# Hybrid attention layer: compressed values' product in fp32r, y made where z is made, the prelude's transposes in another order

## The chip, the core and the metric

The kernel runs on one core of one Trainium2 chip. The metric is the time of one execution on the device in microseconds, lower being better. The core has TensorE (PE, whose weight loads are shown as PEld), VectorE (DVE), ScalarE (ACT), GpSimd (POOL) and SyncE (SP), which issues the transfers (DMA). PSUM holds what PE writes, SBUF holds everything else on the chip.

## What is computed

One decoder layer on a sequence of 512 tokens of width 1024 in float32: a normalisation modulated by a condition c, one wide projection, two groups of attention heads (A: sliding window with sinks; B: three branches over compressed, selected and windowed keys), a gate by SiLU of z, and an output projection added to x.

```python
# D_MODEL 1024, SEQ 512, BATCH 1, HEAD_DIM 64; 8 heads in each group, 2 K/V heads (g) with 4 query heads (r) each
mod = jax.nn.silu(c) @ w_ada + b_ada
shift, scale, gate = jnp.split(mod, 3, axis=-1)
h = rms_norm(x, norm_gain) * (1 + scale[:, None, :]) + shift[:, None, :]
proj = h @ w_in
(q_a, k_a, v_a, z_a, q_b, kc, vc, ks, vs, kw, vw, z_b, g_b) = jnp.split(proj, _split_points(), axis=-1)
...
o_a = banded_gqa(qa, ka, heads(v_a, A_KV), SWA_WINDOW, rel_bias[:, :A_HEADS], sinks)
...
k_cmp = qk_norm(compress_blocks(heads(kc, B_KV), cmp_pos_k, w_cmp_k1, w_cmp_k2), k_gain_cmp)
v_cmp = compress_blocks(heads(vc, B_KV), cmp_pos_v, w_cmp_v1, w_cmp_v2)
...
o_cmp, o_sel = nsa_cmp_sel(qb, k_cmp, v_cmp, k_sel, heads(vs, B_KV), bias_b)
o_win = banded_gqa(qb, k_win, heads(vw, B_KV), NSA_WINDOW, bias_b, None)
gb = jax.nn.sigmoid((g_b + b_nsa_gate).astype(jnp.float32)).reshape(Bn, S, B_HEADS, N_NSA_BRANCHES, 1)
o_b = gb[..., 0, :] * o_cmp + gb[..., 1, :] * o_sel + gb[..., 2, :] * o_win

y = jnp.concatenate([o_a.reshape(Bn, S, D_A) * jax.nn.silu(z_a.astype(jnp.float32)),
                     o_b.reshape(Bn, S, D_B) * jax.nn.silu(z_b.astype(jnp.float32))], axis=-1)
out = y.astype(x.dtype) @ w_out
return x + gate[:, None, :] * out
```

Group B's compressed branch takes 31 overlapping blocks of 32 tokens, runs each through a small MLP to one key and one value of 64 elements per K/V head g, and attends to these. With 512 tokens there are 8 blocks to select from and 16 may be selected, so the selected branch attends to all earlier tokens.

## The kernel before

**Stages.** A prelude up to about 49 us loads x, turns it (x has 4 blocks of 128 tokens; each is transposed on PE in two halves of four 128x128 pieces), computes the modulation, and runs the first projection (q, k and v of group A) over eight blocks k of the model width. From there to about 268 us two streams are interleaved: slots of attention, one for each head row, branch and query block, and the remaining projections, done in pieces in between (L490, L500). Last comes the output projection, eight column blocks n of 24 matmuls with 512 columns (L500; the last n in two halves), each followed by one DVE operation for gate and residual (L1048) and a store.

**Precision.** The large products run in fp32r. Where that is not enough, an operand is split in two fp32r parts, a high part that is its rounded copy and a low part that is what rounding left out, and two or three products are added in PSUM. So weights are split by ACT (wh, L175) and DVE (wl, L176), h into hh and hl, y into yh and yl. Products in plain fp32 are shown in the trace as two records each.

**The compressed branch.** `cmp_mlp` ends in the second layer: keys in one product, values by L648 (four fp32 matmuls, two K/V heads by two halves of the hidden width), where the 32 value rows stand four times below each other in a tile `vc[g]` of 128 rows. `cmp_attn` makes the probabilities and transposes them (L714) into two tables `PTc[g]` (L716), in which rows 32r to 32r+32 belong to head row r. `slot_pv` collects a head row's output `o` in one PSUM bank: the probabilities times values of its slots (L969) and, for group B after the last slot of a head row, the compressed values' product: for each g one fp32 matmul (L975) with 32 rows and 64 output rows:

```python
for g in range(2):
    PE.matmul(o[64 * g:64 * g + 64, :], vc[g][32 * r:32 * r + 32, :],
              PTc[g][32 * r:32 * r + 32, :], start=False, stop=True, skip_group_check=True)
```

**y.** `make_y` (L829, L831, L832) multiplies o by z on DVE (yf), copies to yh on ACT and subtracts to yl on DVE. `post_z` makes z of a pair of heads. For group B, either z is there first and `slot_pv` calls `make_y`, or o is there first: then o is copied (ob, L984) and `make_y` is called in a loop after `stream.drain()`, ahead of the output projection.

**The prelude.** Its instructions stand in each engine in the order of the code (`in_order`). PE transposes x (`x_turned`, L325, into PSUM banks sq and skv), spreads silu(c) (L353), makes the bias lines (L262), the modulation of block 0 in two halves of its contraction (`mod_pe`, L223; e = 0, 1, each with a transfer of its own), spreads the normalisation factor (L376) and sums the modulation's columns (L233). DVE copies the transposed blocks (`x_kept`), scales them by that factor (`scaled`, L278), finishes AB, the modulation's scale and shift (L238, L239), splits the weights' low part (swl, L273) and h's (L287). ACT makes hh (L390 for block 0, L284 for others). For k from 2 on the modulation is done by DVE as two row sums over 1024 columns (L243). In the loop over k, `new_tile(k + 1)` ends with `scaled(k + 3)`. Dummy matmuls on zeros (L320, counts in ND) fill PE's time while it waits for x.

**Order and memory.** Behind the prelude a scheduler of the framework puts each engine's instructions in order, except in blocks that hold PE's order (`block()`); tiles come from rotating pools, so that where they lie is not fixed by hand. `T2` is a pool of NT2 tiles of 128x512. PSUM has eight banks of 128x512 float32.

## Time and profile before

| | us |
|---|---|
| median of 3 runs | 313.62 (313.52 to 313.69) |
| profiled execution | 313.25 |
| its span | 311.4 |
| PE busy in the span | 303.4 (97%) |
| DVE busy | 238.1 (76%) |
| ACT busy | 196.4 (63%) |
| POOL busy | 3.8 (1%) |

The span runs from the first to the last instruction of the profiled execution; what lies around it is in the execution's time but not in the trace. The page's busy shares are means over the whole span. The page's division into 40 slices shows where they differ:

```profile
PE   8899999999999999999999999999999999999995
DVE  3789998999986477787999999986977887445311
ACT  4676367767787676967867658696567777413000
PEclk9999999999999999999999999999999999999999
DMA  7999965890284653041342244005520210034301
```

Each digit is the busy share of 7.8 us in tenths. Rows of the chain of work that ended last show a start, a length, an engine and a line; rows of a line's own view give the least, the median and the greatest duration in nanoseconds, with the first and last start.

### The profile page before, as it was taken

What the parts mean: (1) busy time and instruction counts of PE and PEld (TensorE: products, weight loads), DVE (VectorE), ACT (ScalarE), POOL (GpSimd) and SP (SyncE); (2) the same over time, 40 slices, a digit from 0 to 9 for tenths busy, and PEclk for the clock granted to TensorE, in tenths of its full rate; (3) what the DMA queues carried; (4) which work ended last, traced back from release to release, by engine and by line L of the source; (5) the groups of instructions that cost most, each with busy time, mean ns of one, the idle gap of its engine ahead of it and who ended that gap; (6) DMA issues with size and microseconds to landing.
All of it is one profiled execution on the core that took longest, in us unless ns stands there. A gap on an engine that the chain in (4) does not pass through costs nothing.

```text
span 311.4 us, 5871 instructions
## 1 busy us (share of the span) xinstructions
PE 303.4 (97%) x2131; PEld 253.0 (81%) x2131; DVE 238.1 (76%) x665; ACT 196.4 (63%) x473; POOL 3.8 (1%) x21
## 2 busy tenths in 40 slices
PE   8899999999999999999999999999999999999995
PEld 4578878898988899989978688779788878788885
DVE  3789998999986477787999999986977887445311
ACT  4676367767787676967867658696567777413000
POOL 1000000000000000000000000000000000000000
PEclk9999999999999999999999999999999999999999
DMA  7999965890284653041342244005520210034301
GB/s 262 380 401 290 415 240 199 282 295 14 72 233 140 183 180 113 2 135 36 116 157 68 67 177 144 20 0 212 196 69 0 75 62 2 0 73 148 116 35 69
DMA packets 27420, 44.21 MB, mean 142 GB/s; under 512 B 1712, under 2 KB 19408, under 8 KB 27392
## 3 DMA queue, kind: packets, MB, share of 16 engines
q1 hardware_dynamic: 27392, 43.84, 42.3%
q8 instruction: 17, 0.28, 0.3%
q14 instruction: 11, 0.09, 0.1%
HBM read 41.70 MB, written 2.14 MB: 141 GB/s over the span
## 4 chain that ended last, share of the span: by engine, by line
PE 72%; DVE 19%; ACT 3%; DMA 2%; issue 2%; SPq 0%; DVEq 0%; ACTq 0%
PE pj L500 30%; PE po L969 8%; PE s L894 8%; PE pj L490 7%; DVE ada_ring L243 5%; PE pt L952 4%; PE pt L942 4%; PE s L619 3%; DMA xf<-in_xn 2%; PE sq L294 2%; DVE swl L273 2%; DVE wl L176 1%; PE po L975 1%; DVE hl L287 1%; DVE pa L899 1%
## 5 line engine op out<-in xcount | busy, mean ns | idle before, releaser
L175 ACT ACTIVATE wh<-raw 128x512 fp32r<-128x512 f32 (+1 forms) x52 | 31.4, 630 | 28.0 <-PE pj L500 27.4
L176 DVE TENSOR_TENSOR wl<-raw,wh 128x512 fp32r<-128x512 f32 (+1 forms) x52 | 35.3, 692 | 11.4 <-issue 6.0
L490 PE MATMUL pj<-wl,hh 128*128 128x256 f32 (+1 forms) x128 | 36.7, 287 | 0.1
L490 PE MATMUL pj<-wh,hh 128*128 128x256 f32 (+1 forms) x128 | 36.7, 288 | 0.0
L490 PE MATMUL pj<-wh,hl 128*128 128x256 f32 (+1 forms) x128 | 36.3, 284 | 0.0
L906 ACT ACTIVATE pp<-pp,nm 128x256 f32<-128x256 f32 (+2 forms) x48 | 29.2, 611 | 9.9 <-DVE nm L899 9.5
L500 PE MATMUL pj<-hh,wh 128*128 128x512 f32 x80 | 32.5, 406 | 0.0
L500 PE MATMUL pj<-hh,wl 128*128 128x512 f32 x80 | 31.7, 397 | 0.0
L500 PE MATMUL pj<-hl,wh 128*128 128x512 f32 x80 | 31.6, 395 | 0.0
L899 DVE CUSTOM_DVE_ANT_0 pp<-s,bias 128x256 f32<-128x256 f32 (+2 forms) x48 | 25.2, 550 | 3.2 <-PE s L894 3.0
L500 PE MATMUL pj<-yh,wl 128*128 128x512 f32 (+1 forms) x72 | 26.6, 371 | 0.0
L500 PE MATMUL pj<-yl,wh 128*128 128x512 f32 (+1 forms) x72 | 26.4, 369 | 0.0
L500 PE MATMUL pj<-yh,wh 128*128 128x512 f32 (+1 forms) x72 | 26.2, 369 | 0.0
L490 PEld LDWEIGHTS pj<-wh,hh 128*128 128x128 f32 x128 | 24.0, 188 | 0.6 <-issue 0.3
L490 PEld LDWEIGHTS pj<-wl,hh 128*128 128x128 f32 x128 | 24.1, 188 | 0.4 <-DVE wl L176 0.4
L490 PEld LDWEIGHTS pj<-wh,hl 128*128 128x128 f32 x128 | 24.2, 189 | 0.0
L894 PE MATMUL s<-kTb,qs 128*128 128x256 f32 (+2 forms) x96 | 22.8, 356 | 0.0
L927 DVE TENSOR_SCALAR pp<-pp,rr,grev 128x256 f32<-128x256 f32 (+2 forms) x48 | 21.1, 475 | 0.5
L943 ACT COPY ptT<-pt 128x512 f32<-128x512 f32 (+1 forms) x28 | 15.4, 551 | 4.8 <-PE pt L942 4.3
L500 PEld LDWEIGHTS pj<-hh,wh 128*128 128x128 f32 x80 | 15.1, 188 | 3.9 <-issue 1.3
L953 ACT COPY ptT<-pt 128x384 f32<-128x384 f32 (+1 forms) x32 | 15.6, 530 | 3.9 <-PE pt L952 3.2
L500 PEld LDWEIGHTS pj<-hh,wl 128*128 128x128 f32 x80 | 15.0, 188 | 3.4
(244 smaller groups left out, 696.1 us busy)
## 6 DMA issues: line engine op xcount, KB each, us to landing
ada_ring<-in_w_ada_ss SPq DMA_DIRECT2D x16, 512.0 KB, 9.4
raw<-in_w_cmp SPq DMA_DIRECT2D x8, 512.0 KB, 4.0
raw<-in_w_gate SPq DMA_DIRECT2D x8, 512.0 KB, 7.1
raw<-in_w_o SPq DMA_DIRECT2D x8, 512.0 KB, 3.7
wst_ring<-in_w_qkv_a SPq DMA_DIRECT2D x8, 384.0 KB, 10.0
xr<-in_xT SPq DMA_DIRECT2D x8, 256.0 KB, 2.8
bias<-line_d SPq DMA_DIRECT2D x8, 256.0 KB, 4.2
raw<-in_w_q_b SPq DMA_DIRECT2D x4, 512.0 KB, 4.9
```

What stands on the lines that cost most here:

```text
L175: ACT.activation(wh, src, AF.Copy)
L176: DVE.tensor_tensor(wl, src, wh.bitcast(F32), op=OP.subtract)
L243: DVE.tensor_tensor_reduce(out=w, in0=w, in1=scb, scale=1.0, scalar=init, op0=OP.mult, op1=OP.add, accum_out=out)
L490: PE.matmul(bank[:, t * n:(t + 1) * n], h[:, tb * 128:(tb + 1) * 128], w[:, k % 2, :], start=k == 0 and m == 0, stop=k == 7 and m == 2)
L500: PE.matmul(bank, w, h[:, cols], start=k == 0 and m == 0, stop=k == 7 and m == 2)
L894: PE.matmul(ps, qs[h][:, 128 * i:128 * i + 128], k[:, hl_, lo:lo + n], start=hl_ == 0, stop=hl_ == 1)
L899: DVE.tensor_tensor_reduce(out=P[:, g, 0:w], in0=ps[:, 0:w], in1=bt, scale=1.0, scalar=init, op0=OP.add, op1=OP.min, accum_out=nm[:, g:g + 1])
L906: ACT.activation(P[:, g, 0:e], P[:, g, 0:e], AF.Exp, bias=nm[:, g:g + 1], scale=-1.0, accum_out=dn[:, g:g + 1])
L927: DVE.tensor_scalar(v, v, rr[:, g:g + 1], gates[:, g, br:br + 1], op0=OP.mult, op1=OP.mult)
L943: ACT.copy(T[:, :, 0:nb, :], rev(pt[:, 0:2 * nb * 128].rearrange("p (g b q) -> p g b q", g=2, b=nb)))
L953: ACT.copy(T[:, 0:nb, :], rev(pt[:, 0:nb * 128].rearrange("p (b q) -> p b q", b=nb)))
L969: PE.matmul(o[64 * g:64 * g + 64, 128 * i:128 * i + 128], vb[:, 64 * g:64 * g + 64], sl["T"][g][:, b, :], start=first_of and b == 0, stop= ...
```

## The change

There are three edits and one size.

1. The compressed values' product. The value rows are made once for both K/V heads (L648's loop over g goes), and then twice in tiles `vc_high` and `vc_low` of 128 rows: each holds a 64-column half per g, with rows of the other g set to nought by the factors `of_g`. The probabilities are transposed so that 64 neighbouring rows hold both g of a head row; from these come four tables `PTc[r]`, in which 64 rows are the high part and the other 64 the low part. The product is then two fp32r matmuls of 128 rows by 128 output rows by 512 columns, one with `vc_high`, one with `vc_low`. The layouts of `L` and of the reductions over it follow.
2. `post_z` calls `make_y` where o is there already; the loop after `stream.drain()` goes.
3. The prelude: the second half of x block 2 and four of the eight silu transposes stand ahead of block 3; block 3's second half and its copy stand between the halves of `mod_pe(0)`; `scaled(1)`, `scaled(2)` and `scaled(3)` each come one step earlier, so that `new_tile(1)` no longer calls `scaled(3)`; two dummies move from ahead of block 3 to behind `mod_col(0)`.
4. NT2 goes from 22 to 24.

```diff
@@ -28,6 +28,6 @@
 AHEAD = 6
-NT2 = 22
+NT2 = 24
 WAIT_L, WAIT_M = 4, (0, 8)
 PER_A, PER_B = 3.6, (3.5, 1.6, 7)
-ND = (11, 0, 1, 2)
+ND = (11, 0, 1, 0, 2)
 NR = 4
@@ -123,2 +123,6 @@
     DVE.memset(ones, 1.0)
+    of_g = con.tile([128, 2], F32, name="of_g")
+    POOL.memset(of_g, 0.0)
+    for q in range(4):
+        POOL.memset(of_g[32 * q:32 * q + 32, q % 2:q % 2 + 1], 1.0)
 
@@ -341,2 +345,7 @@
         sqd = stp.tile([128, 512], F32, name="sqd")
+        def silu_rows(g):
+            for j in range(4):
+                PE.transpose(flat_kv[g][:, 128 * j:128 * j + 128],
+                             sc_col[:, 4 * g + j:4 * g + j + 1].to_broadcast([128, 128]), ident)
+
         for tb in range(NB):
@@ -344,4 +353,6 @@
             x_turned(tb, pj_q[tb])
-            if tb < 2:
-                x_turned(tb, (flat_kv[0], pj_q[3])[tb], 1)
+            if tb < 3:
+                x_turned(tb, (flat_kv[0], pj_q[3], pj_q[0])[tb], 1)
+            if tb == 2:
+                silu_rows(0)
             if tb < 3:
@@ -351,5 +362,3 @@
                 DVE.tensor_copy(*x_kept(tb, (flat_kv[0], pj_q[3])[tb], 1))
-        for j in range(8):
-            PE.transpose(flat_kv[j // 4][:, 128 * (j % 4):128 * (j % 4) + 128],
-                         sc_col[:, j:j + 1].to_broadcast([128, 128]), ident)
+        silu_rows(1)
         sx = con.tile([128, NB], F32, name="sx")
@@ -367,3 +376,2 @@
         DVE.tensor_copy(lsb, pj_q[1][0:64, 0:320])
-        x_turned(2, pj_q[0], 1)
         DVE.tensor_copy(*x_kept(2, pj_q[0], 1))
@@ -371,2 +379,4 @@
         next(first_mod)
+        x_turned(3, pj_q[2], 1)
+        DVE.tensor_copy(*x_kept(3, pj_q[2], 1))
         for _ in first_mod:
@@ -377,3 +387,3 @@
         mod_col(0)
-        x_turned(3, pj_q[2], 1)
+        dummies(ND[4], pj_q[3])
         scaled(0, rbp, halves[0:1])
@@ -381,3 +391,3 @@
         scaled(0, rbp, halves[1:2])
-        DVE.tensor_copy(*x_kept(3, pj_q[2], 1))
+        scaled(1, rbp)
         for a in range(2):
@@ -393,3 +403,3 @@
         weights_low(0)
-        scaled(1, rbp)
+        scaled(2, rb)
         h_low(0)
@@ -397,3 +407,3 @@
         weights_low(1)
-        scaled(2, rb)
+        scaled(3, rb)
 
@@ -415,3 +425,3 @@
             weights_low(k + 1)
-            if k < 6:
+            if 1 < k < 6:
                 scaled(k + 2, rb)
@@ -634,3 +644,3 @@
         sT = W2("csT", (128, 2, 64))
-        sTv = W2("csTv", (128, 2, 2, 4, 32))
+        sTv = W2("csTv", (128, 2, 2, 2, 32))
         ptv = pt[:, 0:256].rearrange("p (c n) -> p c n", c=2)
@@ -638,4 +648,4 @@
         for hc in range(2):
-            DVE.tensor_scalar(sTv[:, hc], ptv[:, hc, 64:128].rearrange("p (g n) -> p g n", g=2)[:, :, None, :]
-                              .to_broadcast([128, 2, 4, 32]), 0.5, None, op0=OP.mult)
+            DVE.tensor_scalar(sTv[:, hc], ptv[:, hc, 64:128].rearrange("p (g n) -> p g n", g=2)[:, None, :, :]
+                              .to_broadcast([128, 2, 2, 32]), 0.5, None, op0=OP.mult)
         yield 0.25
@@ -645,9 +655,11 @@
         pv = ps_s.tile([128, 512], F32, name="s")
+        for hc in range(2):
+            PE.matmul(pv[:, 0:64], sTv[:, hc].rearrange("p e g n -> p (e g n)"), w2[:, 1, hc, :],
+                      start=hc == 0, stop=hc == 1)
+        for part in ("high", "low"):
+            vc[part] = mp.tile([128, 2, HD], F32R, name=f"vc_{part}")
         for g in range(2):
-            for hc in range(2):
-                PE.matmul(pv[:, 64 * g:64 * g + 64], sTv[:, hc, g].rearrange("p r n -> p (r n)"), w2[:, 1, hc, :],
-                          start=hc == 0, stop=hc == 1)
-        for g in range(2):
-            vc[g] = mp.tile([128, HD], F32, name=f"vc{g}")
-            ACT.activation(vc[g], pv[:, 64 * g:64 * g + 64], AF.Copy)
+            ACT.activation(vc["high"][:, g], pv[:, 0:64], AF.Copy, scale=of_g[:, g:g + 1])
+            DVE.scalar_tensor_tensor(vc["low"][:, g], pv[:, 0:64], of_g[:, g:g + 1], vc["high"][:, g].bitcast(F32),
+                                     op0=OP.mult, op1=OP.subtract)
         kcn = mp.tile([64, 2, HD], F32, name="kcn")
@@ -673,3 +685,3 @@
         L = [mp.tile([128, 2, 257], F32, name="pa", bufs=3).rearrange("p a b -> p (a b)")[:, 0:512]
-             .rearrange("p (a b c) -> p a b c", a=2, b=2) for _ in range(2)]
+             .rearrange("p (i r g n) -> p i r g n", i=2, r=4, g=2) for _ in range(2)]
         pss = [ps_s.tile([128, 512], F32, name="s"), PJ()]
@@ -689,3 +701,3 @@
             for i in range(NB):
-                DVE.tensor_tensor(L[i // 2][:, i % 2, g].rearrange("p (r n) -> p r n", r=4),
+                DVE.tensor_tensor(L[i // 2][:, i % 2, :, g],
                                   pt[:, 128 * i:128 * i + 128].rearrange("p (r n) -> p r n", r=4),
@@ -694,3 +706,3 @@
         for e in range(2):
-            Lv = L[e].rearrange("p i g (r n) -> p (i g r) n", n=32)
+            Lv = L[e].rearrange("p i r g n -> p (i r g) n")
             m = sm.tile([128, 16], F32, name="cm")
@@ -704,4 +716,5 @@
             DVE.reciprocal(dn, dn)
-            DVE.tensor_tensor(dn.rearrange("p (i h) -> p i h", i=2), dn.rearrange("p (i h) -> p i h", i=2),
-                              gsig[:, 2 * e:2 * e + 2].rearrange("p i (h c) -> p i h c", c=3)[:, :, :, 0], op=OP.mult)
+            dv = dn.rearrange("p (i r g) -> p i r g", i=2, r=4)
+            DVE.tensor_tensor(dv, dv, gsig[:, 2 * e:2 * e + 2].rearrange("p i (g r c) -> p i r g c", g=2, c=3)[..., 0],
+                              op=OP.mult)
             DVE.tensor_tensor(Lv, Lv, dn[:, :, None].to_broadcast([128, 16, 32]), op=OP.mult)
@@ -710,8 +723,12 @@
             yield 0.0
-        for g in range(2):
+        for e in range(2):
             pt = PT()
             for i in range(NB):
-                PE.transpose(pt[:, 128 * i:128 * i + 128], L[i // 2][:, i % 2, g, :], ident)
-            PTc[g] = T2(F32, f"ptc{g}")
-            ACT.activation(PTc[g], pt, AF.Copy)
+                PE.transpose(pt[:, 128 * i:128 * i + 128],
+                             L[i // 2][:, i % 2, 2 * e:2 * e + 2].rearrange("p r g n -> p (r g n)"), ident)
+            for p in range(2):
+                t = PTc[2 * e + p] = T2(F32R, f"ptc{2 * e + p}")
+                own, other = slice(64 * p, 64 * p + 64), slice(64 - 64 * p, 128 - 64 * p)
+                ACT.activation(t[own], pt[own], AF.Copy)
+                DVE.tensor_tensor(t[other], pt[own], t[own].bitcast(F32), op=OP.subtract)
             yield 0.44
@@ -820,2 +837,4 @@
             make_y(n, o_a[n], z)
+        elif ("b", n - 4) in o_a:
+            make_y(n, o_a["b", n - 4], z)
         else:
@@ -973,5 +992,5 @@
             if kind == "b":
-                for g in range(2):
-                    PE.matmul(o[64 * g:64 * g + 64, :], vc[g][32 * r:32 * r + 32, :],
-                              PTc[g][32 * r:32 * r + 32, :], start=False, stop=True, skip_group_check=True)
+                for part in ("high", "low"):
+                    PE.matmul(o, vc[part].rearrange("p g d -> p (g d)"), PTc[r], start=False, stop=part == "low",
+                              skip_group_check=True)
             if kind == "a":
@@ -1032,5 +1051,2 @@
     stream.drain()
-    for r in range(4):
-        if 4 + r not in yh:
-            make_y(4 + r, o_a["b", r], sz[r])
```

On PE, the prelude from the last two blocks of x to the first column sums, before (sq_108 and sq_107 take the halves of block 3, sq_105 block 2's second half, sc_col is silu(c), raw the bias lines, scz the modulation's condition, n_y the normalisation factor):

```order
L325 MATMUL sq_108<-first,xf 128x128 x4
L353 MATMUL skv_109<-first,sc_col 128x128 x4
L353 MATMUL skv_110<-first,sc_col 128x128 x4
L262 MATMUL sq_106<-raw 32x320 x2
L325 MATMUL sq_105<-first,xf 128x128 x4
L223 MATMUL pj<-ada_ring,scz 32x256 x8
L376 MATMUL pj<-first,n_y 128x128 x4
L233 MATMUL pj<-ones,macc 128x1 x2
L325 MATMUL sq_107<-first,xf 128x128 x4
```

and in the changed kernel (lines 4 higher, or 5 lower or 10 higher where code moved; block 2's second half goes to sq_111, block 3's halves to sq_114 and sq_113):

```order
L329 MATMUL sq_111<-first,xf 128x128 x4
L348 MATMUL skv_115<-first,sc_col 128x128 x4
L329 MATMUL sq_114<-first,xf 128x128 x4
L348 MATMUL skv_116<-first,sc_col 128x128 x4
L266 MATMUL sq_112<-raw 32x320 x2
L227 MATMUL pj<-ada_ring,scz 32x256 x4
L329 MATMUL sq_113<-first,xf 128x128 x4
L227 MATMUL pj<-ada_ring,scz 32x256 x4
L386 MATMUL pj<-first,n_y 128x128 x4
L237 MATMUL pj<-ones,macc 128x1 x2
```

Four of the silu transposes and block 2's second half have moved ahead of block 3's first half; block 3's second half has moved from behind the column sums to between the two halves of the modulation.

On DVE, from the copy of the bias lines to the last scaling ahead of the second block's AB, before (xTp is x transposed, and also what `scaled` writes; pj is the bank with the normalisation factor, rb its copy in SBUF):

```order
L367 COPY lsb<-sq_106 64x320
L369 COPY xTp<-sq_105 128x4x128
L278 TENSOR_TENSOR xTp<-xTp,pj 128x256
L238 TENSOR_TENSOR AB<-pj,first 128x1
L239 SCALAR_TENSOR_TENSOR AB<-pj,prm_83,first 128x1
L278 TENSOR_TENSOR xTp<-xTp,pj 128x256
L382 COPY xTp<-sq_107 128x4x128
L273 TENSOR_TENSOR swl<-wst_ring,swh 128x768
L278 TENSOR_TENSOR xTp<-xTp,pj 128x512
L287 TENSOR_TENSOR hl<-hf,hh 128x512
L273 TENSOR_TENSOR swl<-wst_ring,swh 128x768
L278 TENSOR_TENSOR xTp<-xTp,rb 128x512
```

and in the changed kernel, behind the same two copies:

```order
L381 COPY xTp<-sq_113 128x4x128
L282 TENSOR_TENSOR xTp<-xTp,pj 128x256
L242 TENSOR_TENSOR AB<-pj,first 128x1
L243 SCALAR_TENSOR_TENSOR AB<-pj,prm_89,first 128x1
L282 TENSOR_TENSOR xTp<-xTp,pj 128x256
L282 TENSOR_TENSOR xTp<-xTp,pj 128x512
L277 TENSOR_TENSOR swl<-wst_ring,swh 128x768
L282 TENSOR_TENSOR xTp<-xTp,rb 128x512
L291 TENSOR_TENSOR hl<-hf,hh 128x512
L277 TENSOR_TENSOR swl<-wst_ring,swh 128x768
L282 TENSOR_TENSOR xTp<-xTp,rb 128x512
```

The copy of block 3's half has moved ahead of the first scaling, and three scalings of 512 columns, not two, stand behind the first block's two halves and ahead of the second block's AB.

On PE, the end of the attention, before: the last head row's product, and what follows it (yh and yl are the heads' y, wh and wl the weights of the output projection):

```order
L969 MATMUL po<-ptT,vw 64x128 x18
L975 MATMUL po<-ptc_2535,vc_1372 64x512
L975 MATMUL po<-ptc_2569,vc_1374 64x512
L500 MATMUL pj<-yh_2640,wl 128x512
L500 MATMUL pj<-yh_2153,wh 128x512
L500 MATMUL pj<-yl_2154,wh 128x512
L500 MATMUL pj<-yh_2153,wl 128x512
```

and in the changed kernel (yh_3469 and yl_3470 are that head row's own y):

```order
L988 MATMUL po<-ptT,vw 64x128 x18
L994 MATMUL po<-ptc_2582,vc_high 128x512
L994 MATMUL po<-ptc_2582,vc_low 128x512
L510 MATMUL pj<-yh_2447,wh 128x512
L510 MATMUL pj<-yl_2448,wh 128x512
L510 MATMUL pj<-yh_2447,wl 128x512
L510 MATMUL pj<-yh_2654,wh 128x512
L510 MATMUL pj<-yl_2655,wh 128x512
L510 MATMUL pj<-yh_2654,wl 128x512
L510 MATMUL pj<-yh_2783,wh 128x512
L510 MATMUL pj<-yh_3469,wh 128x512
L510 MATMUL pj<-yl_2784,wh 128x512
```

The two fp32 matmuls with 64 output rows have become two of 128; seven matmuls stand between them and the first that reads the last head row's yh.

## The prediction, made before the changed kernel was run

> **What bounds the kernel now.** I began with the page's busy shares and its chain of work that ended last.
>
> ```profile
> PE 303.4 (97%) x2131; PEld 253.0 (81%) x2131; DVE 238.1 (76%) x665; ACT 196.4 (63%) x473; POOL 3.8 (1%) x21
> PE 72%; DVE 19%; ACT 3%; DMA 2%; issue 2%; SPq 0%; DVEq 0%; ACTq 0%
> ```
>
> TensorE is busy for 97% of the span and carries 72% of the chain, but VectorE carries 19%. So the average hides stages with another limit. The table of busy time by stage says where they are.
>
> ```profile
> 20.00:49.00 29.00, 28.26 (x160) 23.91 (x159) 27.77 (x50) 16.41 (x27) 0.00 (x0) 1.00 0.83 299
> 180.00:190.00 10.00, 10.00 (x85) 8.35 (x84) 9.76 (x27) 6.31 (x13) 0.00 (x0) 1.00 0.43 159
> 190.00:200.00 10.00, 10.00 (x83) 8.26 (x83) 9.76 (x34) 7.14 (x22) 0.00 (x0) 1.00 0.34 107
> 200.00:210.00 10.00, 9.96 (x56) 7.38 (x56) 8.76 (x29) 9.15 (x24) 0.00 (x0) 1.00 0.00 0
> 268.00:309.00 41.00, 40.11 (x197) 32.85 (x193) 16.78 (x26) 6.81 (x12) 0.00 (x0) 1.00 0.26 81
> ```
>
> The columns are the stage, then PE, weight loads, DVE, ACT and POOL, then the granted clock, which is 1.00 in all of them. From 20 to 49 us DVE works 27.77 of 29.00 us. From 180 to 268 PE leaves no gap although DVE is nearly full at first: there, time taken off PE counts if DVE can follow. In the tail PE alone counts. I work against the profiled execution's own 313.25 us (span 311.4); the median of the timed runs, 313.62, is 0.37 above it, and I carry the difference over.
>
> **1. The compressed values' product.** The chain and the lines behind it:
>
> ```profile
> 199.99 1.00 PE po L975 x4
> 223.55 1.00 PE po L975 x4
> 249.10 1.00 PE po L975 x4
> 267.61 1.00 PE po L975 x4
> L975 PE MATMUL po<-ptc,vc x16: 587/612/638, 199.9 to 268.0; 32*64 32x512 f32 x16
> 187.17 1.39 PE pj L500 x6
> L500 PEld LDWEIGHTS pj<-hh,wh x80: 186/188/246, 52.8 to 244.8; 128*128 128x128 f32 x80
> ```
>
> Once per head row r the chain pays 1.00 us for L975: two fp32 matmuls, four records. The new form is two fp32r matmuls of 128x128 by 512 columns, the shape of L500, which goes at 1.39 / 6 = 0.232 us each in an unbroken row although each also has a weight load of 188 ns. So 2 x 0.23 = 0.46 per row, 0.54 saved, **2.15 us** over four. Since all four stand on the chain with PE full around them, I count all of it.
>
> A rule that speaks against this: the Trainium skill, "TensorE: Matmul & The Clock Gate", Part 3, section "The mechanism", says that a weight load overlaps running matmuls only where its row group differs, and both new matmuls use all 128 rows. By it each would cost 0.188 + 0.232 = 0.42 us and the four rows would save 0.6 us; the L500 row, with the same row group each time at 0.232 us, disagrees.
>
> The rest of this part:
>
> ```profile
> 108.78 0.61 PE s L648 x6
> L716 ACT ACTIVATE ptc<-pt x2: 580/592/603, 195.6 to 197.7; 128x512 f32<-128x512 f32 x2
> L569 DVE TENSOR_TENSOR kTb<-pt,kTb x8: 682/688/695, 94.1 to 130.3; 64x512 fp32r<-64x512 f32 x8
> ```
>
> At L648 the values' second layer goes from four fp32 matmuls (eight records, 0.10 us each by this row) to two: 0.4 us, on a stretch with waits of PE's own, so I take **0.35** (0.2 to 0.45). Making the tables costs more than before: four DVE subtractions of 64x512 at 0.69 us, 2.76 us in all, and four ACT copies of half the rows where two of 0.592 stood; at most the same 0.59 each, so up to 1.2 us more. Two small operations each on ACT and DVE for vc and five memsets on an idle POOL come long before use. ACT has room (7.14 of 10 us). DVE has 0.24 us free in 190 to 200, then 1.24, so the cover is not DVE's idle time but the queue: PE shows no gap at 97.6% DVE, because transposes stand two slots behind their scores. What is queued behind a subtraction is the softmax of the next slots (L899, L927 before), and PE waits for these if they fall behind that lead. Also the first product needs its subtraction; in the new order 41 other PE instructions stand between the last transpose of the first table and that product, nine of them of L500's size (9 x 0.232 = 2.1 us), against 0.59 + 0.69 us for copy and subtraction. I take **0**, with bounds 0 (all within the lead) and +2.8 (every subtraction on the path). The row nearest to it, PE's 10.00 of 10.00, is why I choose the low end.
>
> **2. Where y is made.** The old tail:
>
> ```profile
> L500 PE MATMUL pj<-hh,wh x80: 392/396/502, 52.9 to 245.0; 128*128 128x512 f32 x80
> 268.66 0.69 DVE L829 SCALAR_TENSOR_TENSOR yf<-po,szb 128x512 f32<-128x512 f32 x1 [3.92 <-PE po L975]
> 269.38 0.63 ACT L831 ACTIVATE yh<-yf 128x512 fp32r<-128x512 f32 x1 [3.22 <-DVE yf L829]
> 269.87 0.68 DVE L829 SCALAR_TENSOR_TENSOR yf<-ob,szb 128x512 f32<-128x512 f32 x1
> 268.61 39.52 PE pj L500 x193
> ```
>
> Two heads' y (three operations each) leave the tail for the z stage. There was nothing to win: PE runs its 193 matmuls in one piece while DVE does this. The two triples add 2 x (0.69 + 0.69) us to DVE somewhere in 200 to 268, where it has over 10 us free. The last head's y stays behind the last product. By the new order seven other matmuls stand between its second half and the first use of its yh: 8 x 0.232 = 1.86 us from that half's start. In this time the half ends (0.39, by the row above), yf is made (from 268.66 to yh's start at 269.38 it is 0.72) and yh (0.63): 1.74, and a few hundredths for each of the three handovers. PE waits 0 to 0.3; I take **+0.2**.
>
> **3. The prelude.** The chain there:
>
> ```profile
> 2.12 7.48 DMA xf<-in_xn
> 9.73 0.63 PE sq L325 x4
> 10.36 0.87 PE skv L353 x8
> 11.23 0.66 PE sq L262 x4
> 11.89 0.59 PE sq L325 x4
> 12.48 1.00 PE pj L223 x16
> 13.48 0.58 PE pj L376 x4
> 14.06 0.59 PE pj L233 x4
> 14.65 0.51 PE sq L325 x4
> 15.19 0.50 ACT hh L390
> L207 SPq DMA_DIRECT2D ada_ring<-in_w_ada_ss x2: 442/448/454, 3.3 to 3.8; - x2
> DMA to landing us min/median/max: 8.0/8.4/8.7
> ```
>
> PE waits for the last block of x until 9.73. After it come eight silu transposes (0.87), the bias lines, block 2's second half (0.59), the modulation (1.00), the column sums, and block 3's second half (0.51), which hh waits for. Now four silu transposes and block 2's half run before 9.73, in the wait: 0.44 + 0.59 off. Block 3's half goes between the halves of the modulation. So its first half starts at 9.73 + 0.63 + 0.43 + 0.66 = 11.45, the moved transposes end near 12.5, and the second half cannot start before the second transfer lands, 3.8 + 8.7 = 12.5 at the latest. Before, it started near 12.9 (8 of 16 records into the 1.00). So the modulation ends 0.3 to 0.4 earlier, and hh, which waited until 15.17 for transposes though AB was done at 14.98 (L239's row below), gains 0.2 more. The two dummies after the column sums stand in PE's slack before hh. I take **-0.4** (-0.2 to -0.6) for the first product.
>
> From 20.8 us on the chain runs on DVE:
>
> ```profile
> 14.77 0.21 DVE L239 SCALAR_TENSOR_TENSOR AB<-pj,prm,first 128x1 f32<-128x1 f32 x1
> 17.07 0.69 DVE L278 TENSOR_TENSOR xTp<-xTp,pj 128x512 f32<-128x512 f32 x1 [0.30 <-ACT rb L391]
> 20.54 0.16 DVE L238 TENSOR_TENSOR AB<-pj,first 128x1 f32<-128x1 f32 x1 [0.47 <-PE pj L233]
> 24.90 0.60 DVE xTp L278
> PE sq L294 <- ACT hh L284: 0.7, 3, 0.3
> ```
>
> Each k costs DVE two row sums (1.20 each in the chain), hl, swl (0.96) and one scaling (0.60), some 4.7 us, and PE waits for it at three of the last k's. One scaling, the 0.60 at 24.90, moves out of this loop to before 20.54, where DVE waited 0.30 and 0.47 us, and the copy ahead of it is out of the way too. Six scalings become five on the path: **-0.6** (0 to -0.7). What is late next is again DVE. The last row bounds it from the other side: PE waits 0.7 us in all for hh in this stage, and no more than that can be had there. The -0.4 passes on to DVE's chain, which begins at 20.54 with PE's column sums.
>
> **Sum:** -2.15 - 0.35 + 0 + 0.2 - 0.4 - 0.6 = -3.3 us; 313.25 becomes 309.95 and the median 313.62 becomes **310.3 us**.
>
> **Rivals.** (a) DVE becomes the bound: the four subtractions and the tables' new dependence push the softmax of the slots near 200 us back by the full 2.76 us, and PE then waits for DVE, so that the product's saving only shortens a PE that waits: -1.0 - 0.35 + 0.2 + 2.8 = +1.65, **315.3 us**, slower. It decides once more than 3.3 us of delay and lost saving reach PE. For it: 9.76 of 10 us busy. Against: PE's gapless stage and DVE's 1.24 us of idle time right after. (b) Each new matmul waits for its own weight load, 0.188 + 0.232 = 0.42 us, 0.84 a row: the products save 4 x 0.16 = 0.64 in place of 2.15, the total is -1.8 and the time **311.8**. Against: L500's 0.232 with the same load. The rule named in part 1 would bring this about. (c) The prelude gives nothing, because later k's wait for transfers: the DMA share is 0.83 in 20 to 49. Then -2.3, **311.3**. Against: no wait in that stage ends with a DMA. (d) The order between 49 and 268 us is made anew in many places, not only in those changed. In 100 to 160 PE is busy 59.30 of 60.00:
>
> ```profile
> 100.00:160.00 60.00, 59.30 (x483) 53.77 (x483) 45.70 (x157) 43.98 (x117) 1.59 (x8) 1.00 0.38 119
> ```
>
> With 0.7 us of gaps there, and short stretches in the chain that run on DVE or ACT, another order can give or take an estimated 1.2 us: **309.1 or 311.5**. (e) The change does not do what it says: the two fp32r matmuls wait for half-tables as long as the fp32 pair took, so the 2.15 is gone: -1.15, **312.5**.
>
> The Trainium skill, "FP8 and Floating Point Precision", section "TensorE Precision Notes", gives true FP32 four passes; two fp32r products in their place would halve 1.00 to an estimated 0.50, which agrees with 0.46 and moves the sum by 0.16 us.
>
> **Chances.** Forecast with (d)'s shifts 0.68, (a) 0.06, (b) 0.08, (c) 0.10, (e) 0.08. The range from 308.6 to 312.6 is the forecast with the low ends of its terms and half of (d) below, and reaches up over (b), (c) and (e); left out are (a), (e) with an adverse order, and a larger gain than summed. A difference of 0.2%, 0.63 us, is about what a measurement of this kernel can tell from none. Of (b), (c) and (e) 0.06 is put to an adverse order that brings them to no change. Faster 0.88, the same 0.06, slower 0.06.
>
> **What would show it.** L994's rows in the chain at 0.46 to 0.5 us four times; the first projection product near 15.3 instead of 15.73, the last k's hh near 47 instead of 47.94; PE still gapless from 180 to 210; the tail again one piece of 39.5 us. Gaps of PE near 195 to 205 ended by DVE would make (a) right; L994 at 0.8 would make (b) right; a first product at 15.3 with an unmoved hh at 47.9, (c).

## The result, and the profile after

The changed kernel takes 309.50 us (median of 4 runs, 309.42 to 310.21) against 313.57 for the kernel before in the same comparison; the ratio is 0.9876 with a 95% interval of 0.9859 to 0.9893, so 3.4 to 4.4 us less. The forecast was 3.3 us less and 310.3; the range, 308.6 to 312.6, held the time. The profiled execution took 309.57 us with a span of 307.7 (before 313.25 and 311.4).

The busy shares and the chain of the changed kernel:

```profile
PE 299.7 (97%) x2119; PEld 252.5 (82%) x2119; DVE 240.2 (78%) x671; ACT 197.0 (64%) x475; POOL 4.6 (1%) x26
PE 72%; DVE 17%; ACT 5%; DMA 3%; issue 2%; SPq 0%
```

PE lost 3.7 us of work, which is the whole change of the span; DVE gained 2.1. The chain of waits of the changed kernel at the places that the prediction spoke of (start, length, engine, line):

```profile
2.12 7.84 DMA xf<-in_xn
...
14.98 0.50 ACT hh L400
15.52 0.50 PE sq L298
...
46.70 0.61 ACT hh L288
47.36 0.50 PE sq L298
...
197.10 0.66 PE po L994 x2
...
222.73 0.66 PE po L994 x2
...
246.48 0.67 PE po L994 x2
...
265.19 0.66 PE po L994 x2
265.85 38.56 PE pj L510 x189
```

The last k's hh comes at 46.70 in place of 47.94, although x block 3 came 0.36 us later in this execution (2.12 + 7.84 = 9.96, before 9.60). The products stand in the chain at 0.66 us in place of 1.00. The tail is again one piece, with 189 matmuls in place of 193: four more were done earlier.

The table of busy time by stage (PE, weight loads, DVE, ACT, POOL, granted clock, DMA):

```profile
20.00:49.00 29.00, 28.74 (x164) 24.84 (x164) 27.46 (x49) 17.84 (x29) 0.00 (x0) 1.00 0.83 304
180.00:190.00 10.00, 10.00 (x76) 8.48 (x71) 9.96 (x31) 6.82 (x16) 0.00 (x0) 1.00 0.28 93
190.00:200.00 10.00, 10.00 (x80) 8.24 (x78) 9.37 (x28) 8.72 (x24) 0.00 (x0) 1.00 0.43 159
200.00:210.00 10.00, 10.00 (x56) 7.87 (x54) 9.81 (x28) 7.16 (x20) 0.00 (x0) 1.00 0.00 1
210.00:220.00 10.00, 10.00 (x90) 8.51 (x90) 9.61 (x32) 7.83 (x26) 0.00 (x0) 1.00 0.88 303
```

The prediction shows the row of before from 200 us on; the next one is:

```profile
210.00:220.00 10.00, 10.00 (x90) 8.76 (x90) 7.39 (x27) 6.66 (x23) 0.00 (x0) 1.00 0.59 211
```

The third number is DVE's busy time. Its idle time behind 200 us (1.24 and 2.61 of 10 before) is filled to 9.81 and 9.61, and PE still shows no gap. Summed over 180 to 220 us DVE has 38.75 us in place of 35.66, 3.1 more, and the four subtractions are 2.76 of work. Which single stage gets the filling also depends on the order: with 24 tiles alone (E4 below), and no subtraction added, DVE is at 9.95 from 200 to 210.

### The profile page after: what moved, and what is told of

The parts are those of the page before. It is cut to its first block, busy times and chain, and to the rows that moved or that the text cites. A ratio compares the mean times of both kernels' runs of the same rounds, so it can differ in the third digit from the quotient of the medians.

```text
span 307.7 us, 5849 instructions
## 1 busy us (share of the span) xinstructions
PE 299.7 (97%) x2119; PEld 252.5 (82%) x2119; DVE 240.2 (78%) x671; ACT 197.0 (64%) x475; POOL 4.6 (1%) x26
## 4 chain that ended last, share of the span: by engine, by line
PE 72%; DVE 17%; ACT 5%; DMA 3%; issue 2%; SPq 0%
PE pj L510 30%; PE po L988 8%; PE s L913 8%; PE pj L500 6%; DVE ada_ring L247 5%; PE pt L971 4%; PE pt L961 3%; PE s L629 3%; DMA xf<-in_xn 3%; PE sq L298 2%; DVE wl L180 2%; DVE swl L277 2%; DVE hl L291 1%; ACT qs L559 1%; DVE qs L560 1%
## 5 line engine op out<-in xcount | busy, mean ns | idle before, releaser
L500 PE MATMUL pj<-wl,hh 128*128 128x256 f32 (+1 forms) x128 | 36.7, 287 | 0.0
L500 PE MATMUL pj<-wh,hh 128*128 128x256 f32 (+1 forms) x128 | 36.7, 286 | 0.0
L500 PE MATMUL pj<-wh,hl 128*128 128x256 f32 (+1 forms) x128 | 36.5, 285 | 0.0
L500 PEld LDWEIGHTS pj<-wh,hh 128*128 128x128 f32 x128 | 24.1, 188 | 0.5 <-ACT pa L925 0.2
L500 PEld LDWEIGHTS pj<-wl,hh 128*128 128x128 f32 x128 | 24.1, 188 | 0.1
L500 PEld LDWEIGHTS pj<-wh,hl 128*128 128x128 f32 x128 | 24.2, 189 | 0.0
L1064 DVE SCALAR_TENSOR_TENSOR fin<-pj,gate,xr 128x512 f32<-128x512 f32 (+1 forms) x9 | 6.2, 691 | 17.0 <-PE pj L510 17.0
L925 ACT ACTIVATE pa<-pa,nm 128x257 f32<-128x257 f32 (+1 forms) x32 | 15.4, 480 | 3.8 <-DVE nm L918 3.4
```

Source lines behind the costliest of these rows:

```text
L500: PE.matmul(bank[:, t * n:(t + 1) * n], h[:, tb * 128:(tb + 1) * 128], w[:, k % 2, :], start=k == 0 and m == 0, stop=k == 7 and m == 2)
L925: ACT.activation(P[:, g, 0:e], P[:, g, 0:e], AF.Exp, bias=nm[:, g:g + 1], scale=-1.0, accum_out=dn[:, g:g + 1])
```

## The experiments

One profiled execution differs from another by the arrival of x block 3, so I read four times off each trace: that arrival (the start of DVE's sum of squares over the block, which waits for it), the first projection product, the last k's first product with its own h, and the start of PE's last matmul. The arrival, the three stretches between, and their sum, in us:

| kernel | arrival | to first product | to last k's product | to PE's last matmul | from arrival to end | median of the runs, and of before beside it |
|---|---|---|---|---|---|---|
| before | 9.62 | 6.11 | 32.86 | 259.24 | 298.22 | 313.57 |
| changed | 9.99 | 5.53 | 31.83 | 256.76 | 294.13 | 309.50 / 313.57 |
| E1 prelude alone | 9.82 | 5.75 | 31.86 | 259.22 | 296.82 | 311.44 / 313.31 |
| E2 product alone, 24 tiles | 10.22 | 5.99 | 32.45 | 258.00 | 296.43 | 311.60 / 313.31 |
| E3 y alone | 9.92 | 6.11 | 32.86 | 259.44 | 298.41 | 313.52 / 313.31 |
| E4 24 tiles alone | 9.31 | 5.99 | 32.46 | 259.93 | 298.38 | 313.55 / 313.31 |
| E5 changed, without y | 9.22 | 5.61 | 31.86 | 258.01 | 295.47 | 310.07 / 312.77 |
| E6 changed, 22 tiles | 9.21 | 5.59 | 31.84 | 257.45 | 294.88 | 309.87 / 312.77 |
| E7 changed, subtractions twice | 8.81 | 5.82 | 31.85 | 257.22 | 294.89 | 309.91 / 312.77 |
| E8 changed, fp32 product | 9.79 | 5.66 | 31.83 | 258.13 | 295.62 | 310.73 / 312.77 |
| E9 scalings alone | 9.10 | 6.17 | 32.25 | 259.27 | 297.69 | 312.44 / 313.00 |
| E10 transposes alone | 10.35 | 5.67 | 32.44 | 259.29 | 297.41 | 312.35 / 313.00 |
| E11 changed, two scalings on GpSimd | 9.87 | 5.67 | 32.28 | 257.11 | 295.05 | 310.64 / 313.00 |
| E12 changed, again | 9.89 | 5.71 | 31.85 | 256.82 | 294.38 | 309.11 / 313.00 |

The arrival lay between 8.81 and 10.35, and shifts everything behind it. (In E6 and E9 DVE started the sum without waiting, so there the block was in place at that time at the latest.) The sixth column leaves the arrival out. It follows the ratios of the timed runs to within some 0.4 us, except for E11, where it is 0.8 us lower than the ratio gives. The fifth column repeats best: before, E1, E9 and E10 have the same code behind the prelude and lie between 259.22 and 259.29, the changed kernel and E12 at 256.76 and 256.82. The median of before differs from one comparison to the next (312.77 to 313.57), so runs that stand beside different medians of before are compared by their ratios (0.001 is 0.31 us).

**E1, the prelude alone.** The hunks of the change from ND to `new_tile`, nothing else.

> Before plus the prelude's edit alone. If the parts add up: 1.0 to 1.25 us faster than before (ratio 0.996 to 0.997), with the last k's hh near 46.7 to 46.9 us, as in the changed kernel. Rival, that a part of the gain comes from the new order of the instructions between 49 and 268 us: that order is again another one here, so the time lies away from this by up to 1 us although hh comes at the same place.

Measured: ratio 0.9949 (0.9934 to 0.9964), 1.1 to 2.1 us faster; from arrival to end 1.40. Behind the prelude nothing moved (259.22 against 259.24), so the order of the middle played no part. A little more than expected; E9 and E10 say where it comes from.

**E2, the product alone.**

```diff
-NT2 = 22
+NT2 = 24
...
-                for g in range(2):
-                    PE.matmul(o[64 * g:64 * g + 64, :], vc[g][32 * r:32 * r + 32, :],
-                              PTc[g][32 * r:32 * r + 32, :], start=False, stop=True, skip_group_check=True)
+                for part in ("high", "low"):
+                    PE.matmul(o, vc[part].rearrange("p g d -> p (g d)"), PTc[r], start=False, stop=part == "low",
+                              skip_group_check=True)
```

> Before plus the compressed values' product alone, with its 24 tiles of T2. If the parts add up: four products at 0.57 in place of 1.06 us from start to start, 2.0, and four records of 0.11 us less in the second layer, 0.45: 2.4 us faster (ratio 0.992), with the last hh at 47.9 as before. If the added subtractions reach PE: less than 1.5 us faster, with gaps of PE behind 190 us. If the new order gives a part: over 2.9 us faster.

Measured: ratio 0.9954 (0.9940 to 0.9967), 1.0 to 1.9 us faster: less than the 2.4 expected. Not for the reason named there: PE's waits behind 190 us hold nothing of the sort, but there is one in the tail, named below. Beside E4, which has the same 24 tiles without the product, it is 1.95 us faster.

**E3, y alone.**

```diff
+        elif ("b", n - 4) in o_a:
+            make_y(n, o_a["b", n - 4], z)
...
-    for r in range(4):
-        if 4 + r not in yh:
-            make_y(4 + r, o_a["b", r], sz[r])
```

> Before plus y made where z is made, alone. Prediction's view: no change, within 0.3 us of before, since PE never waited in the tail. Rival: the two triples of operations cost or free something near 205 to 265 us, where DVE is 75% busy: over 0.5 us either way, with gaps of PE there.

Measured: 1.0007 (0.9998 to 1.0017), no change, as the prediction had it.

**E4, 24 tiles alone.** The one line NT2 = 24.

> Before with 24 tiles of T2 in place of 22 and nothing else. No instruction is added or removed. If the order of the middle is worth nothing: within 0.3 us of before. If a freer pool lets the scheduler place work better: 0.5 us or more faster, and that share has to be taken off the product's gain.

Measured: 1.0010 (0.9999 to 1.0021), no change in sum, but not the same program. In this trace four more matmuls of the output projection run before the attention's end, 189 in place of 193 are left behind it, and PE then waits. The waits between 262 and 275 us (who waited for what, us in total, times, longest):

```profile
PEld pj L500 <- ACT yh L831: 1.4, 1, 1.4
PE pj L500 <- ACT yh L831: 1.0, 1, 1.0
```

and ACT at that place (start, length, ..., idle before and its releaser):

```profile
268.77 0.63 ACT L831 ACTIVATE yh<-yf 128x512 fp32r<-128x512 f32 x1 [3.22 <-DVE yf L829]
270.10 0.63 ACT L175 ACTIVATE wh<-raw 128x512 fp32r<-128x512 f32 x1 [0.69 <-PE pj L500]
270.63 1.14 ACT L831 ACTIVATE yh<-yf 128x512 fp32r<-128x512 f32 x2
```

The scheduler put a weight split between the first yh and the other two. The split waits 0.69 us for a buffer that PE is still reading, and two yh, whose yf DVE has made by 269.93, wait behind it until 270.63, while PE runs out of matmuls that need neither. E2's trace has the same pair of rows, 1.4 and 1.0 us. Whether the four matmuls less or the place of the split weighs more, no run separates.

**E5, the changed kernel without the y edit.** E3's hunks taken back.

> The changed kernel without the y edit: the two triples stand behind the attention again. In the run of the product alone and in the run with 24 tiles alone PE stood 1.00 us in the tail, waiting for a yh that ACT made only after a weight split. Theory: with 24 tiles the y edit is worth that stall, so this kernel is 1.0 to 1.4 us slower than the changed one (ratio to before about 0.991 to 0.992), with a PE wait of 1 us for yh near 268 us. Rival: it is worth nothing in company either, as it was alone: within 0.3 us of the changed kernel.

Measured: ratio to before 0.9911 (0.9896 to 0.9926) against 0.9876 and, for E12, 0.9873: some 1.1 us slower than the changed kernel; behind the prelude 258.01 against 256.76, 1.25. The chain of waits of E5 at the end of the attention:

```profile
264.50 0.68 PE po L992 x2
265.18 0.02 issue
265.20 1.90 DVE yf L846 x3
267.11 0.05 issue
267.16 0.02 ACTq L848
267.17 0.43 issue
267.60 0.62 ACT yh L848
268.23 0.04 issue
268.27 6.89 PE pj L510 x28
```

PE has left the chain for three yf and a yh, and waits 1.00 us at 268.27 for the yh, as expected. In the changed kernel the same place is one PE piece of 38.56 us, and PE shows no wait of its own there. So the y edit alone is worth nothing and is worth more than 1 us in company.

**E6, the changed kernel with 22 tiles.**

> The changed kernel with 22 tiles of T2. If the two tiles only hold the two added tables and the order they bring is worth nothing: within 0.4 us of the changed kernel. If 22 tiles make PE wait for a free one near 190 to 205 us, where four tables are alive, not two: 0.5 to 2 us slower.

Measured: 0.9902 (0.9887 to 0.9917), by the ratios 0.8 to 0.9 us slower than the changed kernel and E12, with intervals that overlap. The trace is 0.69 us longer behind the prelude (0.63 against E12), ten times what two profiles of one program differ by there, so a loss of some 0.7 us is likely, though the timed runs alone don't settle it. It is not the wait for a tile that the expectation named. PE's one wait of 160 to 262 us in the table of waits is for DVE:

```profile
PE pt L971 <- DVE pp L946: 0.3, 1, 0.3
```

So two tiles more lose 0.69 us behind the prelude in the kernel before (E4), and win about as much here, where the late y are gone.

**E7, the subtractions made twice.**

```diff
                 DVE.tensor_tensor(t[other], pt[own], t[own].bitcast(F32), op=OP.subtract)
+                DVE.tensor_tensor(t[other], pt[own], t[own].bitcast(F32), op=OP.subtract)
```

> The changed kernel with each of the four table subtractions made twice (the same result): 2.76 us more on DVE between 190 and 200 us, where it is over 94% busy. If the lag stays hidden by the lead of the scores over the transposes: within 0.4 us of the changed kernel. If DVE sets PE's pace there (the slower rival of the prediction): 1 to 2.8 us slower, with PE gaps ended by DVE between 195 and 215.

Measured: 0.9907 (0.9893 to 0.9921); by the ratios 1.0 us slower than the changed kernel and 1.1 than E12, with intervals that touch or overlap; the trace is 0.46 us longer behind the prelude, out of 2.76 us added. The stages of E7 and a line of its waits:

```profile
190.00:200.00 10.00, 10.00 (x77) 8.12 (x76) 9.62 (x26) 5.53 (x18) 0.00 (x0) 1.00 0.43 159
200.00:210.00 10.00, 9.84 (x53) 7.65 (x52) 9.70 (x25) 8.61 (x20) 0.00 (x0) 1.00 0.08 20
210.00:220.00 10.00, 10.00 (x88) 8.44 (x88) 9.97 (x32) 6.62 (x18) 0.00 (x0) 1.00 0.74 243
...
PE pj L510 <- ACT ob L1004: 0.2, 1, 0.2
```

DVE is now full to 220, and PE shows its first gap, 0.16. It ends with ACT, not with DVE: ACT's copy ob came late, because the table copy ahead of it had waited 1.45 us for the doubled subtraction. Over all four table copies ACT waits 3.3 us so in E7 and 0.4 us in the changed kernel. So this run adds a wait of ACT besides the work on DVE, and does not price DVE's load alone. The lag is hidden for the most part, 1.7 to 2.3 us of 2.76; a second 2.76 us begins to show.

**E8, the new layout in fp32.** One product of 64 rows by 128 output rows, no split of tables or values.

```diff
-                for part in ("high", "low"):
-                    PE.matmul(o, vc[part].rearrange("p g d -> p (g d)"), PTc[r], start=False, stop=part == "low",
-                              skip_group_check=True)
+                own = slice(64 * (r % 2), 64 * (r % 2) + 64)
+                PE.matmul(o, vc[0][own].rearrange("p g d -> p (g d)"), PTc[r // 2][own], start=False, stop=True,
+                          skip_group_check=True)
```

> The changed kernel with the new layout but without the split: per head row one fp32 product of 64 rows by 128 output rows, two ACT copies of a whole table, no subtractions, one value tile. It tells precision from layout. If the gain is that of fp32r: two records of about 0.5 us, 1.0 per row in place of 0.57, so 1.7 us slower than the changed kernel (ratio to before about 0.993). If the old product's cost came from its two column halves: within 0.4 us of the changed kernel. If the subtractions cost PE something: less than 1.7 slower, with PE's order otherwise alike.

Measured: 0.9930 (0.9918 to 0.9943), by the ratios 1.7 us slower than the changed kernel and 1.8 than E12, as expected for fp32r. The chain of E8 has the product four times like this:

```profile
196.67 1.05 PE po L988 x2
```

One fp32 product of 128 output rows costs about what two of 64 output rows each, side by side, did (1.00). So the layout alone saves nothing, and the gain is that of fp32r. From the product's start to the next instruction's E8 takes 1.05 and the changed kernel 0.57, four times 0.48 is 1.9; the trace is only 1.37 longer behind the prelude. By the traces, whose orders are not quite alike, the split's work on DVE and ACT may so cost the changed kernel half a microsecond; the timed runs, at 1.7 to 1.8, show next to nothing of it, though their intervals leave room for it.

**E9 and E10, the two halves of the prelude.** E9 has only the scalings:

```diff
         DVE.tensor_copy(*x_kept(3, pj_q[2], 1))
+        scaled(1, rbp)
...
-        scaled(1, rbp)
+        scaled(2, rb)
...
-        scaled(2, rb)
+        scaled(3, rb)
...
-            if k < 6:
+            if 1 < k < 6:
                 scaled(k + 2, rb)
```

E10 has the other hunks of the prelude (ND, `silu_rows`, the transposes and the copy of block 3's half).

> Before plus the earlier scalings alone: one of DVE's six scalings of 0.60 us leaves the loop over k, the transposes stay where they were. Theory: 0.6 us faster (ratio 0.998), first product as before, last hh 0.6 us earlier; up to 0.95 if the pause of 0.34 us that DVE showed ahead of the third block's weight subtraction in the runs with 22 tiles goes too. Rival, that PE's first product sets everything: no change.

> Before plus the moved transposes and dummies alone. Theory: first product 0.4 to 0.5 us earlier, counted from the arrival of x block 3 (5.4 to 5.6 us after its first transpose in place of 6.0), and all later ones with it: 0.3 to 0.5 us faster (ratio 0.9985). Rival: the second half of the first modulation's weights lands too late and takes the gain back: no change.

Measured: E9 0.9979 (0.9969 to 0.9989), 0.66 us; from first product to the last k's 32.25 in place of 32.86, 0.61. E10 0.9983 (0.9973 to 0.9992), 0.53 us; to the first product 5.67 in place of 6.11, 0.44. But E10 also gained 0.42 between the first and the last product, where it changes nothing. Of this 0.34 is a pause of DVE. Before:

```profile
28.55 0.16 DVE L250 TENSOR_TENSOR AB<-modt,first 128x1 f32<-128x1 f32 x1
29.05 0.96 DVE L273 TENSOR_TENSOR swl<-wst_ring,swh 128x768 fp32r<-128x768 f32 x1 [0.34 <-issue]
```

E10 at the same place:

```profile
28.84 0.16 DVE L250 TENSOR_TENSOR AB<-modt,first 128x1 f32<-128x1 f32 x1
28.91 0.96 DVE L273 TENSOR_TENSOR swl<-wst_ring,swh 128x768 fp32r<-128x768 f32 x1
```

The pause of 0.33 to 0.34 us stands ahead of this one instruction in the profiles of before, E3 and E9, and in none of the others. In before no releaser is named; in E3 and E9 it is a landing of `ada_ring`, a tile that this instruction does not read. What it is stays open.

**E11, two scalings on GpSimd.** An attempt at a faster kernel: PE still waits for the last hh in the changed kernel.

```diff
-            DVE.tensor_tensor(y[k][:, c], xT[k][:, c], by[:, c], op=OP.mult)
+            (POOL if k > 5 else DVE).tensor_tensor(y[k][:, c], xT[k][:, c], by[:, c], op=OP.mult)
```

> The changed kernel with the last two scalings (k = 6 and 7) on GpSimd, which is idle there, so that DVE's chain in the loop is 1.2 us shorter. Theory: PE waits 0.4 us for the last hh in the changed kernel, and that wait goes: 0.3 to 0.5 us faster than the changed kernel. Rival: GpSimd's work slows DVE's or is late itself: no change or slower.

Measured: 0.9924 (0.9912 to 0.9936), 310.64 us, 1.5 above E12 in the same comparison. GpSimd takes 1.73 us for each scaling, and starts the first at 17 us, as soon as ACT has made rb. E11's DVE in that time, with GpSimd's group ahead (least, median, greatest ns; first and last start):

```profile
L282 POOL TENSOR_TENSOR xTp<-xTp,rb x2: 1727/1730/1732, 17.0 to 18.7; 128x512 f32<-128x512 f32 x2
...
17.58 1.69 DVE L291 TENSOR_TENSOR hl<-hf,hh 128x512 fp32r<-128x512 f32 x1
19.19 2.04 DVE L277 TENSOR_TENSOR swl<-wst_ring,swh 128x768 fp32r<-128x768 f32 x1
```

and E12's:

```profile
17.64 0.69 DVE L291 TENSOR_TENSOR hl<-hf,hh 128x512 fp32r<-128x512 f32 x1
18.38 0.96 DVE L277 TENSOR_TENSOR swl<-wst_ring,swh 128x768 fp32r<-128x768 f32 x1
```

DVE lost 1.00 and 1.08 us on two operations beside GpSimd's, more than the 1.2 us that left its chain, and it lost them ahead of the loop, where PE then waited 0.9 us for hh. From arrival to end the traces differ by 0.67 us only; where the rest of the 1.5 lies they don't show. The Trainium skill, "GPSIMD Engine Reference", section "1. Specifications", says that GpSimd's SBUF interfaces are shared with VectorE, with contention for instructions that have two SBUF inputs. Both slowed operations have two, and the trace agrees with that. A third DVE operation with two SBUF inputs, the scaling that began at 16.88, just ahead of GpSimd's first at 17.0, kept its 0.69 us.

**E12, the changed kernel again.**

> The changed kernel as it is, once more, beside the others of this call: 309.3 to 309.8 us. It tells how far one profiled execution differs from another: the arrival of x block 3 lay between 9.3 and 10.2 us in the profiles so far, and the whole program shifts with it.

Measured: 309.11 us, below the 309.3 to 309.8 expected, but beside a before of 313.00 in place of 313.57; the ratio, 0.9873 (0.9859 to 0.9888), agrees with the first comparison's 0.9876. From arrival to end it is 294.38 against 294.13. The arrivals so far had in fact lain between 8.81 and 10.22. A difference of a quarter of a microsecond between two profiles of one program, once the arrival is taken out, is what the table can't tell from none.

## Why the prediction was right, point by point

**The product: right in mechanism, 2.15 a little large.** From the start of the product to that of the next instruction it was 1.00 us (199.91 to 200.92 in the timeline) and is now:

```profile
197.03 0.19 PEld L994 LDWEIGHTS po<-ptc,vc_high 128*128 128x128 f32 x1 [0.17 <-DVE nm L918]
197.03 0.50 PE L994 MATMUL po<-ptc,vc_high 128*128 128x512 f32 x1
...
197.14 0.19 PEld L994 LDWEIGHTS po<-ptc,vc_low 128*128 128x128 f32 x1
...
197.37 0.39 PE L994 MATMUL po<-ptc,vc_low 128*128 128x512 f32 x1
...
197.60 0.27 PE L961 MATMUL pt<-first,pp 128*128 128x128 f32 x1
```

0.57, not 0.46: the second half goes at 0.23 as the row of L500 had it, but the first, behind the products with 64 output rows, takes 0.34. Its own weight load starts with it, at 197.03, and not under the matmul before it, as the second's does. A matmul of before that had waited for hh, with its load at the same moment (43.88), also takes 0.33 to the next start (44.21), so the 0.11 more looks like a load without cover; no run tests that. With 0.57 the four products save 4 x 0.43 = 1.7. E2 against E4, which differ in this edit alone, give 259.93 - 258.00 = 1.93 us behind the prelude, with the second layer and the subtractions in it. The forecast for the three was 2.5. Rival (b) fails with these rows: 0.57 is not 0.84, and the second half's weights were loaded from 197.14 on, while the first half ran. By the rule that the prediction cited from the Trainium skill, "TensorE: Matmul & The Clock Gate", Part 3, section "The mechanism", that load should have waited; the same section, though, also lets a load for the background weight buffer go ahead of running matmuls. The measurement decides. Rival (e) falls with the same rows. E8 shows that the gain is fp32r's.

**The second layer: right in the count.** Four records stand where eight stood. In before six of the eight take 0.61 us of the chain, in the changed kernel each pair takes 0.17; no run has this edit alone.

**The subtractions: hidden, or nearly: 0 to 0.5 where I had 0.** By the traces E8, without them, lacks half a microsecond of the loss that its products should bring; by the timed runs it lacks next to nothing. E7, with twice as many, loses 0.5 by the trace and 1.0 by the ratios. Rival (a) was right that DVE would be full, but in the changed kernel PE shows no gap that DVE ends: of 2.76 us 2.2 or more stay covered.

**Where y is made: wrong, and so was leaving the pool's size out.** The prediction took +0.2 because there was "nothing to win: PE runs its 193 matmuls in one piece". That reads the tail of the schedule before, and E3 confirms it for that schedule. But the changed kernel has another: 24 tiles alone let four more output matmuls go earlier (E4) and put a weight split ahead of two late yh, and a wait of 1.0 us opens. E4 against before is +0.69 behind the prelude; the y edit against E5 is -1.25. Together -0.56, where I had +0.2. The sum has no term for the pool; rival (d), which allowed 1.2 us either way for a new order, is the only place of the prediction where such a thing fits. The last product's own y costs PE next to nothing, at the low end of my 0 to 0.3: PE has no wait there, only its weight loads do (0.3 and 0.2).

**The prelude: right, and 0.4 us too small by the traces.** -0.4 for the first product measured -0.44 alone (E10) and -0.58 and -0.40 in the changed kernel's two profiles. -0.6 for the scaling measured -0.61 (E9). From first to last k's product 32.86 became 31.83, 1.03: the rest, 0.42, is for the most part the pause of 0.34 on DVE, which was in the profile before and which I had put into no step. It went with the change, as it went in E10 and E4. The bound that the prediction took from PE's waits for hh, 0.7 us and no more, was a misreading: a wait is counted from the end of the record before it, and the loss is more. From 43.37 to 43.88 lie 0.51 us between two starts where an unbroken row has 0.12 (44.21 to 44.33), and only 0.23 of the 0.39 lost is shown as a wait. Rival (c) falls with hh at 46.70.

**The sum.** -3.8 to -4.1 by the two profiles from arrival to end, in place of -3.3; the parts: product, second layer and subtractions -1.9 (forecast -2.5), order and y -0.56 (+0.2), first product -0.4 to -0.6 (-0.4), DVE's loop -0.61 (-0.6), the pause -0.4 (not seen). The errors partly cancel: 0.6 us that the product fell short stand against 0.76 and 0.4 that were not foreseen. That the sum came within a microsecond is in part luck; that the gain lies in the product and the prelude was foreseen for the right reasons. The parts alone, E1, E2 and E3, give 1.40 + 1.79 - 0.19 = 3.0 us from arrival to end, and the pause of 0.4 is in both E1 and E2, so 2.6; the changed kernel has 3.8 to 4.1, and the rest, 1.2 to 1.5, is about the stall that the y edit takes away (1.25), which only exists in company.

## What to carry to other kernels

A change that a profile prices at nothing is priced for one schedule. Where a scheduler makes the order anew, ask of each stage whose last wait is covered by little work what happens when some of that work moves ahead; here, with two spare tiles, four matmuls moved and a weight split came ahead of late work, and an edit worth nothing became worth a microsecond. Price a pool's size as an edit of its own, with the other edits and without them. And before moving work to an idle engine, look for what the two share: two scalings of 1.73 us on GpSimd cost DVE 2.1 us, where on DVE they would have been 1.2 us of its chain.

## What the runs showed of the hardware

- A scaling of 128x512 takes 1.73 us on GpSimd, 0.69 on DVE; two DVE operations of two inputs begun beside it took 1.69 and 2.04 in place of 0.69 and 0.96; one begun just ahead of it kept its 0.69 (E11, E12).
- A product of 128 output rows right behind products of 64 takes 0.34 us to the next start, and its weight load starts with it; the one after it, loaded under it, takes 0.23 (changed kernel). Behind a wait for hh it is 0.33 as well (before, 43.88 to 44.21).
- An fp32 product with 128 output rows and 512 columns takes 1.05 us (E8), about as long as two of 64 side by side (1.00, before).
- The transfer of x block 3 is in place between 8.81 and 10.35 us in the fourteen profiles, and the program behind it shifts with it.
